# One tiny transfer issued by SyncE ahead of the first load of a batched matrix product

## The chip, the core and the metric

The kernel runs on one core of a Trainium2 chip. The metric is device time in microseconds (us) from launch to the last result in memory. A profiled execution also has a span, from the core's first to its last instruction.

## The reference

For each of 32 batch entries, a 256 x 512 matrix is multiplied by a 512 x 384 matrix, in float32:

```python
batch, dim_i, dim_j, dim_k = 32, 256, 512, 384
def reference(x, y):
    return np.einsum('bij,bjk->bik', x, y).astype(np.float32)
```

The inputs are 16.8 MB (x) and 25.2 MB (y), the output is 12.6 MB.

## The kernel before

**Tiling.** The 32 batch entries are taken in N = 8 groups of Q = 4. One group fills all 128 partitions, 32 partitions per entry. `load_x(n)` (line 67) brings the four x matrices of group n as one transfer of 128 rows of 16,384 bytes (2,048 KB). `load_y(n)` (line 71) brings the four y matrices as one transfer of 128 rows of 24,576 bytes (3,072 KB). Both inputs have two buffers, `x_sb[0..1]` and `y_sb[0..1]`, used by even and odd groups. The whole output of the core stays in one large tile `o_sb` until it is stored.

**Stages of one group.** GpSimd casts x (`round_x`, line 126) and y (`round_y`, line 136) from float32 to float16. VectorE transposes x blocks (line 156), TensorE multiplies (line 217) into PSUM, and ScalarE and VectorE copy the results from PSUM to `o_sb` (line 165). There is no planner: each engine's order is written out by hand, and the engines meet at semaphores.

**Transfers.** All of them are issued by SyncE, in one queue, which the profile calls q1. Four loads are issued at once, before the program branches to its bodies:

```python
for ins in (load_y(0), load_x(0), load_x(1), load_y(1)):
    tc.no_tile_sem_insts.add(ins.ins.name)
```

The other twelve loads (lines 98 to 102) each wait until the casts have emptied the buffer they write. Then come three stores (line 96): groups 0 to 4, groups 5 and 6, and group 7. `s_out` counts the landings of the stores, 16 for each transfer. The last instruction of the body waits for all of them and sets the semaphore back:

```python
sp.wait_op(s_out, 16 * 3, "sem-ge").then_inc(s_out, -16 * 3)
```

**What the steps below touch.** SyncE's order at the start (line 75), the queue q1 behind it, `s_out`, and everything that waits for `s_y[0]`: `round_y(0)` (line 136) is the first consumer of loaded data.

Of the kernel before, what the change touches and what calls it, by code (L numbers as in the profile page):

```python
# [9 lines left out]
F32 = mybir.dt.float32  # L10
P = 128
Q = 4
# [7 lines left out]
def kernel(  # L20
# [6 lines left out]
    nc = tc.nc  # L27

    B, I, J = x.shape
# [10 lines left out]
    def sbuf(name, shape, dtype):  # L40
        return nc.alloc_sbuf_tensor(name, shape, dtype).ap()
# [5 lines left out]
    xt_sb = sbuf("xt_sb", [P, TW, P], F32)  # L47
    y_r = sbuf("y_r", [P, T, K], MM_DT)
    spare = sbuf("spare", [1, 1], F32)
    o_ps = nc.alloc_psum_tensor("o_ps", [P, NE * Q, 512], F32).ap()  # L50

    s_x = [nc.alloc_semaphore(f"s_x{n}") for n in range(N)]
# [9 lines left out]
    s_out = nc.alloc_semaphore("s_out")  # L62
# [4 lines left out]
    def load_x(n):  # L67
        src = x[n * Q : (n + 1) * Q].rearrange("g (p r) j -> (g p) r j", r=R)
        return nc.sync.dma_start(out=x_sb[n % 2], in_=src).then_inc(s_x[n], 16)

    def load_y(n):
        src = y[n * Q : (n + 1) * Q].rearrange("g (q t) k -> (g q) t k", t=T)
        return nc.sync.dma_start(out=y_sb[n % 2], in_=src).then_inc(s_y[n], 16)

    for ins in (load_y(0), load_x(0), load_x(1), load_y(1)):
        tc.no_tile_sem_insts.add(ins.ins.name)
    tc.close()
    tc.compile()  # L78
# [12 lines left out]
    sp = nc.sync  # L91
# [16 lines left out]
    sp.wait_ge(s_dve, NE)  # L108
    store(N - 1, N)
    sp.sem_inc(s_sp, 1)  # L110
    sp.wait_op(s_out, 16 * 3, "sem-ge").then_inc(s_out, -16 * 3)

# [101 lines left out]
    def product(ps, w, m, start, stop, g):  # L216
        return te.add_instruction(  # L217
            mybir.InstMatmult(
                name=nc.get_next_instruction_name(),
                start_tensor_calc=start,  # L220
                stop_tensor_calc=stop,
                tile_size=(PQ, P),
                tile_position=(PQ * g, 0),
                engine=mybir.EngineType.PE,
                ins=[te.lower_ap(m), te.lower_ap(w)],
                outs=[te.lower_ap(ps)],
            )
        )

    xt = xt_sb.bitcast(MM_DT).rearrange("p t (m c) -> p t m c", c=2)  # L230
    with te.Fori(0, N):
        with te.Fori(0, NE) as e:
            take(s_act)
            take(s_dve)
            for t in range(T):
# [3 lines left out]
                for g in range(Q):  # L239
                    s = slice(g * PQ, (g + 1) * PQ)  # L240
                    ins = product(
                        o_ps[:, e * Q + g, :K],
                        xt[s, t // 2, :, t % 2],
                        y_r[s, t],
                        t == 0,
                        t == T - 1,
                        g,
                    )
# [32 lines left out]
```

## Time and profile before

| | us |
|---|---|
| median of 3 runs | 132.0 |
| lowest, highest | 131.71, 132.05 |
| the profiled execution, its own time | 132.13 |
| span of the profiled execution | 130.8 |

The 1.33 us between the profiled execution's time and its span lie outside the first and last instruction. The profile's rows that matter are quoted in the prediction. In the second part of the page the span is cut into 40 equal slices of 3.27 us and each digit is a share in tenths. "DMA" is the mean busy share of the core's 16 DMA engines. A row of the view by windows gives, for a stretch of the span, the busy time of each compute engine with the number of instructions in brackets, the granted TensorE clock, the DMA share and the rate in GB/s. The DMA share and the rate of a window count every packet that starts in it, with its whole duration and all of its bytes, so that a very short window shows one packet alone.

### The profile page before, as it was taken

The numbers are of one execution on the slowest core, as the hardware profiler recorded it, in microseconds if no ns is written. First come the engines' busy times: TensorE is split into PE (matmuls) and PEld (weight loads), VectorE is DVE, ScalarE is ACT, GpSimd is POOL, SyncE is SP. The second block draws the span as 40 slices with busy tenths as digits, with TensorE's granted clock in tenths as the row PEclk, the third lists the DMA queues.
The fourth block names the chain that finished last, engine by engine and source line by source line (L and its number), as shares of the span: only waits on it lengthen the run. The fifth ranks groups of instructions, "written<-read, shape, count | busy, mean of one in ns | idle before, by whom it ended". The sixth has DMA issues, their size and how long they took to land. (4 is left out here: it accounts for less than half of the span.)

```text
span 130.8 us, 3199 instructions
## 1 busy us (share of the span) xinstructions
PE 61.4 (47%) x1024; PEld 46.7 (36%) x1024; DVE 82.7 (63%) x144; ACT 84.1 (64%) x178; POOL 74.2 (57%) x42
## 2 busy tenths in 40 slices
PE   0000009910992589089329905980975499100000
PEld 0000009800991566046129604970953236000000
DVE  0000036899379999985997997599999957920000
ACT  0400000599659989993998899399999957994000
POOL 0006991199929965992899459758973970000000
PEclk9999999995589689977986985599599959965555
DMA  5999999999999999999999999999999999999995
GB/s 120 451 396 441 421 431 451 443 408 428 451 413 421 438 443 401 436 436 443 423 458 398 443 408 466 398 418 436 463 398 408 427 438 425 436 428 421 425 440 248
DMA packets 3379, 54.55 MB, mean 417 GB/s; under 512 B 304, under 2 KB 304, under 8 KB 304
## 3 DMA queue, kind: packets, MB, share of 16 engines
q1 hardware_dynamic: 3376, 54.53, 98.1%
q14 instruction: 3, 0.02, 0.0%
HBM read 41.94 MB, written 12.58 MB: 417 GB/s over the span
## 5 line engine op out<-in xcount | busy, mean ns | idle before, releaser
L165 ACT COPY o_sb<-o_ps (+1 forms) x176 | 82.6, 469 | 31.7 <-PE o_ps L217 29.6
L217 PE MATMUL o_ps<-y_r,xt_sb 32*128 32x384 f16 x1024 | 61.4, 384 | 50.4 <-PEq L214 49.5
L217 PEld LDWEIGHTS o_ps<-y_r,xt_sb 32*128 32x128 f16 x1024 | 46.7, 107 | 64.6 <-issue 56.8
L156 DVE STREAM_TRANSPOSE xt_sb<-x_r 128x256 f32<-128x256 f32 x64 | 38.1, 626 | 30.9 <-POOL x_r L126 18.4
L136 POOL CAST y_r<-y_sb 128x1536 f16<-128x1536 f32 (+1 forms) x22 | 44.3, 2049 | 15.8 <-DMA y_sb<-in_y_dram 15.3
L165 DVE COPY o_sb<-o_ps 32x384 f32 (+1 forms) x80 | 44.6, 557 | 1.6
L126 POOL CAST x_r<-x_sb 128x2048 f16<-128x2048 f32 x16 | 30.2, 1893 | 16.8 <-DVE o_sb L165 12.1
L202 ACT ACT_TABLE_LOAD x1 | 1.3, 1283 | 3.4 <-PEq L78 3.4
L265 POOL MEMSET const-float32-0.0<- 128x1 f32 x1 | 0.1, 98 | 0.2 <-issue 0.2
L202 ACT COPY spare<-const-float32-0.0 1x1 f32<-1x1 f32 x1 | 0.2, 190 | 0.0
L265 POOL MEMSET const-bfloat16-1.0<- 128x1 bf16 x1 | 0.1, 101 | 0.0
L265 POOL MEMSET const-uint8-127<- 128x1 uint8 x1 | 0.1, 101 | 0.0
L265 POOL MEMSET const-float32-1.0<- 128x1 f32 x1 | 0.1, 98 | 0.0
## 6 DMA issues: line engine op xcount, KB each, us to landing
y_sb<-in_y_dram SPq DMA_DIRECT2D x8, 3072.0 KB, 16.8
x_sb<-in_x_dram SPq DMA_DIRECT2D x8, 2048.0 KB, 17.0
out_dram<-o_sb SPq DMA_DIRECT2D x1, 7680.0 KB, 33.9
out_dram<-o_sb SPq DMA_DIRECT2D x1, 3072.0 KB, 17.3
out_dram<-o_sb SPq DMA_DIRECT2D x1, 1536.0 KB, 11.5
```

Of the source, the lines that this page charges most:

```text
L126: po.tensor_copy(x_r[:, e], x_sb[n % 2][:, e * H : (e + 1) * H]).then_inc(s_cast, 1)
L136: ins = po.tensor_copy(y_r[:, s], y_sb[n % 2][:, s])
L156: v.transpose(xt_w[:, w], words[:, e, w]).then_inc(s_xt, 1)
L165: ins = copy(o_sb[g * PQ : (g + 1) * PQ, n, e, h], o_ps[h * PQ : (h + 1) * PQ, e * Q + g, :K],)
L202: a_.copy(spare, nc.const_aps.tensor(0.0, [1, 1], F32))
L217: return te.add_instruction(mybir.InstMatmult(name=nc.get_next_instruction_name(), start_tensor_calc=start, stop_tensor_calc=stop, tile_si ...
L265: nc = _bacc.Bacc("TRN2", target_bir_lowering=False, num_devices=1)
```

## The change

SyncE issues one more transfer as its first instruction. It reads 16 rows of 64 bytes from group 0 of y, 128 rows of y apart, and writes them to a new tile `ahead` of 16 partitions, which nothing reads. It counts on `s_out`, so the final wait asks for 64 instead of 48. The tile is allocated behind all others in the on-chip memory, so no other tile moves. No other instruction of any engine changes or changes its place.

```diff
     spare = sbuf("spare", [1, 1], F32)
+    ahead = sbuf("ahead", [16, 16], F32)
     o_ps = nc.alloc_psum_tensor("o_ps", [P, NE * Q, 512], F32).ap()
...
-    for ins in (load_y(0), load_x(0), load_x(1), load_y(1)):
+
+    first = nc.sync.dma_start(
+        out=ahead, in_=y.rearrange("b j k -> (b j) k")[0 : Q * J : Q * J // 16, :16]
+    ).then_inc(s_out, 16)
+    for ins in (first, load_y(0), load_x(0), load_x(1), load_y(1)):
         tc.no_tile_sem_insts.add(ins.ins.name)
...
-    sp.wait_op(s_out, 16 * 3, "sem-ge").then_inc(s_out, -16 * 3)
+    sp.wait_op(s_out, 16 * 4, "sem-ge").then_inc(s_out, -16 * 4)
```

## The prediction

> **What bounds the kernel now.** I read the page first, for the shares by engine and the 40 slices, and look for an engine that is never idle.
>
> ```profile
> span 130.8 us, 3199 instructions
> PE 61.4 (47%) x1024; PEld 46.7 (36%) x1024; DVE 82.7 (63%) x144; ACT 84.1 (64%) x178; POOL 74.2 (57%) x42
> DMA  5999999999999999999999999999999999999995
> ...
> q1 hardware_dynamic: 3376, 54.53, 98.1%
> ...
> y_sb<-in_y_dram SPq DMA_DIRECT2D x8, 3072.0 KB, 16.8
> ...
> out_dram<-o_sb SPq DMA_DIRECT2D x1, 3072.0 KB, 17.3
> ```
>
> No compute engine is busy for more than 64% of the span. The DMA engines are at nine tenths or more in every slice but the first and the last. So the transfers bound the kernel. The view by windows says how the stream begins, runs and ends:
>
> ```profile
> core 0: us, PE busy (x) PEld busy (x) DVE busy (x) ACT busy (x) POOL busy (x), PEclk, DMA share, GB/s
> 0.00:1.75 1.75, 0.00 (x0) 0.00 (x0) 0.00 (x0) 0.00 (x0) 0.20 (x4) 1.00 0.00 0
> 1.75:2.75 1.00, 0.00 (x0) 0.00 (x0) 0.00 (x0) 0.00 (x0) 0.00 (x0) 1.00 1.70 393
> ...
> 2.75:3.25 0.50, 0.00 (x0) 0.00 (x0) 0.00 (x0) 0.00 (x0) 0.00 (x0) 1.00 0.00 0
> 4.25:10.00 5.75, 0.00 (x0) 0.00 (x0) 0.00 (x0) 0.67 (x2) 0.00 (x0) 1.00 1.00 430
> 10.10:10.90 0.80, 0.00 (x0) 0.00 (x0) 0.00 (x0) 0.00 (x0) 0.03 (x1) 1.00 0.91 389
> 3.25:129.25 126.00, 61.38 (x1024) 46.75 (x1024) 82.69 (x144) 84.10 (x178) 73.96 (x38) 0.82 1.00 429
> 130.30:130.31 0.01, 0.00 (x0) 0.00 (x0) 0.00 (x0) 0.00 (x0) 0.00 (x0) 0.50 0.06 0
> 130.31:130.80 0.49, 0.00 (x0) 0.00 (x0) 0.00 (x0) 0.00 (x0) 0.00 (x0) 0.50 0.00 0
> ```
>
> From 3.25 to 129.25 us the share is 1.00. Nothing is idle there that later work could use to catch up. The time is therefore the moment at which the engines get going, plus a fixed stream, plus a short tail. A microsecond that is lost or won at the start should arrive undiminished at the end. The other condition is that no transfer is issued too late. Here the median y load lands 16.8 us after its issue, while 3.146 MB at 430 GB/s take only 7.3 us: some 9 us of other packets stand ahead of it. The last store is covered as well, as SyncE's timeline shows:
>
> ```profile
> 109.82 9.80 SPq L96 DMA_DIRECT2D out_dram<-o_sb  x2
> ```
>
> These are the last two stores. The row begins with the issue of the second and ends at 109.82 + 9.80 = 119.62 us with the issue of the third. The second (3,072 KB) lands 17.3 us after its issue, near 127.1 us. So the third is queued some 7.5 us before the engines would run dry, and the compute chain ahead of it may be late by that much for nothing.
>
> **The start, packet by packet.** In 1.75 to 2.75 us 393 GB/s for 1 us are 393 KB, that is 16 packets of 24,576 bytes: one first packet of `load_y(0)` for each engine. Their durations add to 1.70 x 1.00 x 16 = 27.2 us, so one takes 1.70 us. In 4.25 to 10.00 us, 430 x 5.75 = 2,472 KB are 101 packets for 1.00 x 5.75 x 16 = 92 us, so one takes 0.91 us. The first packet of an engine thus costs 0.79 us more than a later one. Windows of 10 ns pick single ones out:
>
> ```profile
> 1.83:1.84 0.01, 0.00 (x0) 0.00 (x0) 0.00 (x0) 0.00 (x0) 0.00 (x0) 1.00 9.93 2458
> 1.95:1.96 0.01, 0.00 (x0) 0.00 (x0) 0.00 (x0) 0.00 (x0) 0.00 (x0) 1.00 13.38 2458
> 1.98:1.99 0.01, 0.00 (x0) 0.00 (x0) 0.00 (x0) 0.00 (x0) 0.00 (x0) 1.00 13.28 2458
> 2.55:2.56 0.01, 0.00 (x0) 0.00 (x0) 0.00 (x0) 0.00 (x0) 0.00 (x0) 1.00 9.43 2458
> ```
>
> Each holds one packet (2458 GB/s for 10 ns are 24.6 KB), and share x 0.01 x 16 is its duration: 1.59, 2.14, 2.12 and 1.51 us. They end near 3.42, 4.09, 4.11 and 4.06 us. So the slowest engines begin their steady run 0.7 us after the quickest.
>
> **The change part by part.** It removes nothing. It adds one issue on SyncE, 16 data packets and 16 semaphore packets in q1, one more count for the last wait, and it moves SyncE's first four loads behind the new issue.
>
> ```profile
> 0.74 0.39 SPq L73 DMA_DIRECT2D y_sb<-in_y_dram  x1
> 1.18 0.90 SPq L69 DMA_DIRECT2D x_sb<-in_x_dram  x2
> 2.12 0.53 SPq L73 DMA_DIRECT2D y_sb<-in_y_dram  x1
> 20.27 0.33 SPq L69 DMA_DIRECT2D x_sb<-in_x_dram  x1
> ```
>
> *The issue.* SyncE issues in order and its first issue starts at 0.74 us. The second starts at 1.18, so the price of standing in front is 0.44 us. Bounds are 0.33 us (the issue at 20.27) and 0.53 us (the one at 2.12). I take 0.44, since it is the first issue of the same engine in the same place. `load_y(0)` then moves from 0.74 to 1.18, and its first packets, which started just behind 1.75 us (no window before that holds one), come near 2.2 us. What waits for y, GpSimd's first cast and all behind it, moves with it by the same 0.44 us, and so do the later loads, which wait for those casts; by the 9 us in which a load queues, that is covered. Two x loads and `load_y(1)` are issued 0.44 us later too. These cost nothing, as 3,072 KB of y stand in front of them; if that cover were gone, it would be the same 0.44 us.
>
> *The packets.* A semaphore packet costs 0.06 x 0.01 x 16 = about 0.01 us (window 130.30 to 130.31). No row shows a packet of 64 bytes. At 27 GB/s, the rate of an engine in the steady windows (430/16), it would be 2 ns, and an isolated first one may cost as much as the whole excess, 0.79 us. Between these ends the question is what the excess is. It may be the time in which an idle engine waits for its first data. Then the tiny packet has it and `load_y(0)`, coming 0.44 us later with its own request, has it again, side by side: net +0.44 us. Or it may be a cost of an engine's very first packet alone. Then the tiny packet pays for it while SyncE is still issuing, and the net is 0.44 - 0.79 = -0.35 us. For the latest engines, whose excess is 2.14 - 0.91 = 1.23 us, it is -0.79 us. Or the two follow strictly one after the other, and the net is up to 0.44 + 0.79 = +1.23 us. The trace has one row on new addresses. The first packets of `load_x(0)`, in 10.10 to 10.90 us, take 0.91 x 16 / 389 = 0.0374 ns per byte, against 16 / 430 = 0.0372 before them. So an address that is new does not by itself cost a running engine anything. It does not say whether an engine with one 64-byte packet behind it counts as running. I take the first reading, as it needs no state that outlives a packet.
>
> The Trainium skill, on the page "Perfetto Trace Analysis" (section "DMA Instruction — HWDGE (DVE, Sync)"), speaks against the change: the closing semaphore write of a transfer goes out only after the write before it is confirmed. If the engine's later packets were held meanwhile, it would be the strictly serial case below. The steady windows disagree: semaphore packets stand among their data packets, and the share is still 1.00.
>
> *The final wait and the tile.* The tiny transfer lands over 100 us before the last wait looks at `s_out`, so 64 costs what 48 did. Nothing else is touched.
>
> *The sum.* Span 130.8 + 0.44 = 131.24 us, plus the 1.33 us around it (132.13 - 130.8) makes 132.57 us, which is +0.44 on the profiled execution. That execution stands 0.13 us above the median of 132.0. On the median it makes 132.4 us.
>
> **The rivals.**
>
> *The engines are woken early (faster).* The mechanism is that the excess is paid once per engine, at its first packet, and the tiny transfer pays it. For: the excess is large, it appears nowhere else in 126 us, and the latest three engines of the start, not the mean, have the most to win. Against: the four packets above started up to 0.7 us apart and still finished in two bunches, near 3.4 and 4.1 us, so part of it is waiting and not a fee. Net -0.35 us by the mean and -0.79 us for the latest engines, so 131.65 to 131.2 us; about 131.4. It decides from a fee above 0.44 us on.
>
> *The delay is absorbed (no change).* If all engines wait for something which the first request sets going, the tiny transfer sets it going at the old moment, 1.75 us. `load_y(0)` at 2.2 us would still be in time, since the early engines' data flows only from 3.42 - 0.91 = 2.5 us on. Net 0: 132.0 us. It speaks for this that a packet which started at 2.55 ended no later than one that started at 1.98. The same time would come out if the transfer did not do what it says, but hit only a few of the engines and left the issue hidden.
>
> *Strictly one after the other (slower still).* The tiny packet keeps each engine until its data are written and told. The trace's measure of the latter is the tail: from the last semaphore packet at 130.30 to the end, 0.5 us. The engines are then free at 1.75 + 0.79 + 0.5 = 3.04 us in place of 1.75, and pay the first excess again: +1.3 us, 133.3 us; with half of it overlapped, 132.7. Against it stand the steady windows, where nothing is held.
>
> **How the numbers follow.** The one-to-one delay has a chance of 0.44, the woken engines 0.29, the absorbed delay 0.12, the serial case 0.15. About 0.3% (0.4 us) is what a measurement of this kernel can tell from no change. The delay of 0.44 us lies just above that bound, so I give three quarters of its chance to slower (0.33) and a quarter to same (0.11). The serial case is slower throughout (0.15). Of the woken engines 0.25 is faster, 0.04 same. The absorbed delay is same (0.12). So faster 0.25, same 0.27, slower 0.48. The likeliest case alone spans 132.2 to 132.6 (bounds of the issue, 0.33 to 0.53, and the spread of the runs shown). The range reaches to 131.3 for most of the woken case and to 132.9 for the half-overlapped serial case; left out are the far ends of both.
>
> **What would show it.** Right: SyncE's timeline shows the new issue near 0.74 us and `load_y(0)` near 1.18; the window of the first 24 KB packets begins near 2.2 us; their mean stays near 1.7 us; and the steady share begins 0.4 us later than 3.25. Woken engines would show first y packets near 0.9 us and a steady run that begins no later than before. An absorbed delay would show means near 1.3 us. The serial case would show first packets from 2.6 us on or later. The forecast is wrong if the first y packets end earlier than 3.4 to 4.1 us, or if the end does not move with the start.

## The result, and the profile after

The changed kernel takes 132.40 us (median of 22 runs, 132.28 to 133.13) against 132.01 us for the kernel before (22 runs, 131.71 to 132.59). The ratio is 1.0034, with a 95% interval of 1.0023 to 1.0045: it is slower by 0.30 to 0.59 us, and the forecast was 132.4 us.

The page of the profiled execution (132.40 us) shows a picture much like the one before:

```profile
span 131.1 us, 3200 instructions
PE 65.2 (50%) x1024; PEld 52.9 (40%) x1024; DVE 82.4 (63%) x144; ACT 84.1 (64%) x178; POOL 74.1 (57%) x42
DMA  4899999999999999999999999999999999999996
...
q1 hardware_dynamic: 3408, 54.53, 97.9%
...
ahead<-in_y_dram SPq DMA_DIRECT2D x1, 1.0 KB, 1.5
```

There is one instruction more, 32 packets more (3,408 against 3,376), and the DMA row is nine tenths or more from the third slice to the last but one. It differs from the row before at its two ends: 4 and 8 where 5 and 9 stood, and 6 where 5 stood. The stream lies later by a part of a slice. SyncE's timeline (start, duration, issue) shows by how much:

```profile
0.74 0.39 SPq L77 DMA_DIRECT2D ahead<-in_y_dram  x1
1.19 0.41 SPq L74 DMA_DIRECT2D y_sb<-in_y_dram  x1
1.65 0.90 SPq L70 DMA_DIRECT2D x_sb<-in_x_dram  x2
```

The tiny transfer has taken the place at 0.74 us, and the first load is issued at 1.19 instead of 0.74: 0.45 us later. The windows of the changed kernel (last two columns: DMA share and GB/s) show the rest of the start:

```profile
1.70:2.00 0.30, 0.00 (x0) 0.00 (x0) 0.00 (x0) 0.00 (x0) 0.00 (x0) 1.00 0.06 4
2.20:3.20 1.00, 0.00 (x0) 0.00 (x0) 0.00 (x0) 0.00 (x0) 0.00 (x0) 1.00 1.55 393
3.20:3.65 0.45, 0.00 (x0) 0.00 (x0) 0.00 (x0) 0.00 (x0) 0.00 (x0) 1.00 0.00 0
3.65:129.65 126.00, 65.22 (x1024) 52.91 (x1024) 82.42 (x144) 84.10 (x178) 73.85 (x38) 0.82 1.00 429
```

The 16 tiny packets and their 16 semaphore packets all start in 1.70 to 2.00 us and take 0.06 x 0.30 x 16 = 0.29 us together, 9 ns each. They are gone before the first packets of y appear. Those 16 (393 KB in 1 us) start from 2.20 us on, where they had started from 1.75 on, and take 1.55 us on average (1.55 x 1.00 x 16 / 16), against 1.70 us before. The steady stretch of 126 us has the same share (1.00) and the same rate (429 GB/s) as before. How much later the stream lies is shown by windows of 10 ns, the first of the kernel before, the other two of the changed one:

```profile
3.41:3.42 0.01, 0.00 (x0) 0.00 (x0) 0.00 (x0) 0.00 (x0) 0.00 (x0) 1.00 5.76 2458
3.65:3.66 0.01, 0.00 (x0) 0.00 (x0) 0.00 (x0) 0.00 (x0) 0.00 (x0) 1.00 5.70 2458
130.57:130.58 0.01, 0.00 (x0) 0.00 (x0) 0.00 (x0) 0.00 (x0) 0.00 (x0) 0.50 0.06 0
```

The first packet behind the first 16 starts at 3.65 us instead of 3.41, and the last semaphore packet at 130.57 us instead of 130.30. In this pair of executions the stream is 0.24 us late at its start and 0.27 us late at its end, so nothing was caught up in between. That is less than the 0.45 us of the issue; the first packets, shorter by 0.15 us on average, would account for most of the difference. Between the medians it is 0.39 us.

The compute engines did not carry the delay to the end. The row of the last two store issues ends at 110.20 + 9.30 = 119.50 us with the issue of the last one, against 119.62 us before:

```profile
110.20 9.30 SPq L101 DMA_DIRECT2D out_dram<-o_sb  x2
```

TensorE was busy 3.8 us longer than before (65.2 against 61.4 us), but that does not go with the time: two_ahead below is slower still and has 61.2 us.

### The profile page after: what moved, and what is told of

Its sections match the earlier page's. It is cut to its first block, busy times and chain, and to the rows that moved or that the text cites. A ratio compares the mean times of both kernels' runs of the same rounds, so it can differ in the third digit from the quotient of the medians.

```text
span 131.1 us, 3200 instructions
## 1 busy us (share of the span) xinstructions
PE 65.2 (50%) x1024; PEld 52.9 (40%) x1024; DVE 82.4 (63%) x144; ACT 84.1 (64%) x178; POOL 74.1 (57%) x42
## 3 DMA queue, kind: packets, MB, share of 16 engines
q1 hardware_dynamic: 3408, 54.53, 97.9%
## 5 line engine op out<-in xcount | busy, mean ns | idle before, releaser
L222 PE MATMUL o_ps<-y_r,xt_sb 32*128 32x384 f16 x1024 | 65.2, 405 | 46.9 <-PEq L219 43.7
L222 PEld LDWEIGHTS o_ps<-y_r,xt_sb 32*128 32x128 f16 x1024 | 52.9, 112 | 58.8 <-issue 52.4
```

What stands on the lines that cost most here:

```text
L222: return te.add_instruction(mybir.InstMatmult(name=nc.get_next_instruction_name(), start_tensor_calc=start, stop_tensor_calc=stop, tile_si ...
```

## The experiments

Three theories were to be told apart. *Issue time:* the price is the time that SyncE spends on one more issue ahead of the first load. *Packets:* it is the 32 additional packets or the count on `s_out`. *Waking:* a part of what the issue costs is given back, because the tiny transfer takes the engines' first excess on itself (1.55 against 1.70 us looked like it). In each group the kernels were compared with runs of the kernel before on the same chip. For the first four kernels below the kernel before had a median of 131.96 us, for the other four 131.97 us. The diffs are cut to the lines that matter. In them `tiny(engine)` issues the tiny transfer on the named engine.

**behind_y0: the same transfer, issued second.**

```diff
-    for ins in (first, load_y(0), load_x(0), load_x(1), load_y(1)):
+    for ins in (load_y(0), tiny(nc.sync), load_x(0), load_x(1), load_y(1)):
```

> The same tiny transfer, but issued second, behind load_y(0). Theory 1 (the price is SyncE's issue time in front of the first load): load_y(0) is issued at 0.74 us again, its first packets start near 1.77 us, and the time is that of before, 132.0 us (within 0.15), although x(0), x(1) and y(1) are issued 0.44 us later. Theory 2 (the price is the 32 extra packets and the one more count on s_out): the time stays at 132.4 us.

It took 132.06 us, ratio 1.0008 [0.9999, 1.0017]: not different from before. Timeline and window of this kernel:

```profile
0.74 0.39 SPq L74 DMA_DIRECT2D y_sb<-in_y_dram  x1
1.19 0.41 SPq L78 DMA_DIRECT2D ahead<-in_y_dram  x1
1.66 0.94 SPq L70 DMA_DIRECT2D x_sb<-in_x_dram  x2
```

```profile
1.75:2.75 1.00, 0.00 (x0) 0.00 (x0) 0.00 (x0) 0.00 (x0) 0.00 (x0) 1.00 1.68 393
```

The packets and the count are all there, and so is the 0.45 us of issue, now in front of the x loads (1.66 against 1.18 us). Only the first load is back at 0.74 us, and the time is back too. So behind the first load the packets cost nothing that can be measured (at most 0.22 us by the interval), and here an issue costs time only in front of the transfer that starts the stream.

**two_ahead: two tiny transfers ahead of the first load.**

```diff
-    for ins in (first, load_y(0), load_x(0), load_x(1), load_y(1)):
+    for ins in (tiny(nc.sync, ahead), tiny(nc.sync, ahead2), load_y(0), load_x(0), load_x(1), load_y(1)):
```

> Two tiny transfers ahead of load_y(0). Theory 1 (issue time): load_y(0) is issued near 1.64 us (0.74 + 2 x 0.45), the first 24 KB packets start near 2.65 us, the time is 132.0 + 2 x 0.42 = 132.85 us. Rival (a part of the first packets' excess is a fee that the first tiny transfer has already paid, which is why after is 0.39 and not 0.45): the second one saves nothing more, so it adds its full 0.45 and the time is 132.4 + 0.45 = 132.85 too, with a mean first y packet as in after (1.55 us); if the mean falls again to about 1.4 us, the saving is not a fee but overlap with waiting.

It took 133.02 us, ratio 1.0086 [1.0072, 1.0100], which is 0.95 to 1.32 us slower. Its timeline and window:

```profile
0.74 0.86 SPq L80 DMA_DIRECT2D ahead<-in_y_dram  x2
1.65 0.41 SPq L74 DMA_DIRECT2D y_sb<-in_y_dram  x1
```

```profile
2.65:3.65 1.00, 0.00 (x0) 0.00 (x0) 0.00 (x0) 0.00 (x0) 0.00 (x0) 1.00 1.69 393
```

The first load is 0.91 us late (1.65 - 0.74), which is just below the interval; a little more was lost than the delay alone. The mean first packet is back at 1.69 us. If a tiny transfer saved the excess, two would not save less than one, so the 1.55 us of the changed kernel does not look like one.

**ahead_from_act: the tiny transfer in ScalarE's queue, SyncE as before.**

```diff
-    for ins in (first, load_y(0), load_x(0), load_x(1), load_y(1)):
+    for ins in (tiny(nc.scalar), load_y(0), load_x(0), load_x(1), load_y(1)):
```

> The tiny transfer issued by ScalarE in its own queue at the start, SyncE's order as before. Theory 1 (issue time on SyncE): load_y(0) at 0.74 us again and the time is 132.0 us (within 0.15). If both issues share one descriptor generator, one holds the other up and part of the 0.44 us comes back (132.0 to 132.4 us). Rival (waking pays): the engines have their first packet a little earlier than y's, mean first y packet under 1.5 us, time under 131.8 us.

It took 132.06 us, ratio 1.0006 [0.9997, 1.0016]. The timeline, and the issues with their time to landing:

```profile
0.74 0.39 SPq L73 DMA_DIRECT2D y_sb<-in_y_dram  x1
0.74 0.41 ACTq L78 DMA_DIRECT2D ahead<-in_y_dram  x1
1.19 0.90 SPq L70 DMA_DIRECT2D x_sb<-in_x_dram  x2
```

```profile
ahead<-in_y_dram ACTq DMA_DIRECT2D x1, 1.0 KB, 5.0
```

```profile
0.00:1.75 1.75, 0.00 (x0) 0.00 (x0) 0.00 (x0) 0.00 (x0) 0.20 (x4) 1.00 0.00 0
1.75:2.75 1.00, 0.00 (x0) 0.00 (x0) 0.00 (x0) 0.00 (x0) 0.00 (x0) 1.00 1.83 393
2.75:3.30 0.55, 0.00 (x0) 0.00 (x0) 0.00 (x0) 0.00 (x0) 0.00 (x0) 1.00 0.00 0
```

Both engines issue at 0.74 us, the first load loses nothing, and neither does the kernel. The tiny transfer lands 5.0 us after its issue, against 1.5 us when it stood first. By the windows (the last rows), y's 16 first packets make up the 393 KB of 1.75 to 2.75 us, and nothing else starts before 3.30. So the tiny packets came after y's first ones here and could not have woken anything. The run bears out the issue time and says nothing on waking.

**wait_for_landing: a wait for the tiny transfer's landing.**

```diff
     ).then_inc(s_out, 16)
+    nc.sync.wait_ge(s_out, 16)
```

> The tiny transfer ahead, and SyncE waits for its landing before it issues load_y(0). Theory A (the excess of the first packets is the wait of an empty engine for its first data, paid whenever the engine is empty): load_y(0) is issued near 0.74 + 1.5 = 2.2 us, its first packets start near 3.25 us and take 1.6 to 1.7 us again on average; time 132.0 + 1.5 = 133.5 us. Theory B (it is a fee of an engine's first packet alone): the first y packets take about 0.95 us, time 133.5 - 0.75 = 132.8 us.

This one missed its aim. The wait came to stand at `load_x(0)`, behind `load_y(0)`, as SyncE's waits show (waited in total, times, longest):

```profile
SPq L70 <- DMA ahead<-in_y_dram: 0.6, 1, 0.6
```

```profile
1.19 0.41 SPq L74 DMA_DIRECT2D y_sb<-in_y_dram  x1
2.23 0.92 SPq L70 DMA_DIRECT2D x_sb<-in_x_dram  x2
```

So `load_y(0)` was issued at 1.19 us as in the changed kernel (the second fence is its timeline), and only the x loads were later, at 2.23 us. It took 132.48 us, ratio 1.0037 [1.0024, 1.0051], as the changed kernel did. It shows at least that x loads a further 0.6 us late cost nothing behind 3,072 KB of y.

**landed_first and loads_in_body: the wait where it was meant to be, and its control.** The four first loads move into SyncE's body; in landed_first they stand behind the wait, in loads_in_body there is no tiny transfer.

```diff
-    for ins in (first, load_y(0), load_x(0), load_x(1), load_y(1)):
-        tc.no_tile_sem_insts.add(ins.ins.name)
+    tc.no_tile_sem_insts.add(first.ins.name)
...
+    sp.wait_ge(s_out, 16)
+    load_y(0)
+    load_x(0)
+    load_x(1)
+    load_y(1)
     for n in range(2, N):
```

> The wait for the tiny transfer's landing again, this time in front of load_y(0): in wait_for_landing the wait came to stand behind that load, at load_x(0). Here the four first loads are issued in SyncE's body, behind the wait. Theory A (the excess of the first packets is the wait of an empty engine for its first data): load_y(0) near 2.25 us, first packets near 3.3 us, mean duration 1.55 to 1.85 us as in all runs so far; time 132.0 + 1.5 = 133.5 us. Theory B (a fee of an engine's first packet alone, which the tiny one has paid): mean near 0.95 us, time near 132.8 us.

> The control of landed_first: no tiny transfer, the four first loads in SyncE's body. Both theories: load_y(0) is issued behind the branch, near 1.2 to 1.6 us, mean first y packet near 1.7 us, time 132.0 plus the delay of the issue (132.5 to 132.9 us).

landed_first took 133.62 us, ratio 1.0127 [1.0109, 1.0146]. Its timeline and windows:

```profile
0.74 0.39 SPq L77 DMA_DIRECT2D ahead<-in_y_dram  x1
2.40 0.35 SPq L74 DMA_DIRECT2D y_sb<-in_y_dram  x1
```

```profile
1.70:2.20 0.50, 0.00 (x0) 0.00 (x0) 0.00 (x0) 0.28 (x1) 0.00 (x0) 1.00 0.03 2
3.35:4.45 1.10, 0.00 (x0) 0.00 (x0) 0.00 (x0) 0.06 (x1) 0.00 (x0) 1.00 1.46 357
```

Here every engine's tiny packet was over by 2.20 us and its landing was known before y was issued, a full second start 1.66 us after the first. The 16 first packets of y (357 x 1.10 = 393 KB) still take 1.46 x 1.10 x 16 / 16 = 1.61 us. The excess is thus no fee for an engine's first packet of all. It comes back, on average, when the empty engines get their first large packets. The whole 1.66 us is lost at the end (1.44 to 1.93 us by the interval).

The control took 132.70 us, ratio 1.0049 [1.0034, 1.0064], with its first load at 1.39 us:

```profile
1.39 0.39 SPq L73 DMA_DIRECT2D y_sb<-in_y_dram  x1
```

That is a delay of 0.65 us without any tiny transfer, and 0.45 to 0.84 us are lost. The loss goes with the delay, whatever makes it.

**one_row and rows_128: what the issue costs by the number of rows.**

```diff
-        out=ahead, in_=y.rearrange("b j k -> (b j) k")[0 : Q * J : Q * J // 16, :16]
+        out=ahead[0:1], in_=y.rearrange("b j k -> (b j) k")[0:1, :16]
```

rows_128 has `[0 : Q * J : Q * J // 128, :16]` and a tile of 128 partitions in its place.

> The transfer ahead reads one row of 64 bytes in place of 16, so that it runs on one engine. If the price is a fixed time of an issue: load_y(0) still near 1.19 us, time 132.4 to 132.45 us as with 16 rows. If it goes by the number of packets: load_y(0) near 0.8 us, time 132.0 us.

> The transfer ahead reads 128 rows of 64 bytes in place of 16, 8 packets for each engine. If the price is a fixed time of an issue: load_y(0) near 1.19 us and 132.4 to 132.5 us. If it goes by packets, or if small packets hold the engines, clearly above 132.6 us.

One row took 132.41 us, ratio 1.0028 [1.0018, 1.0039]; 128 rows took 132.41 us, ratio 1.0032 [1.0021, 1.0043]. The timelines of one_row and of rows_128:

```profile
0.74 0.35 SPq L77 DMA_DIRECT2D ahead<-in_y_dram  x1
1.14 0.37 SPq L74 DMA_DIRECT2D y_sb<-in_y_dram  x1
```

```profile
0.74 0.39 SPq L77 DMA_DIRECT2D ahead<-in_y_dram  x1
1.18 0.42 SPq L74 DMA_DIRECT2D y_sb<-in_y_dram  x1
```

The first load is issued at 1.14 and at 1.18 us. From 1 to 128 rows the price of standing in front stays between 0.40 and 0.45 us. It is a price per issue. The queue's packets in one_row and in rows_128 are these:

```profile
q1 hardware_dynamic: 3378, 54.53, 97.3%
q1 hardware_dynamic: 3520, 54.54, 97.7%
```

Against 3,376 before, that is 2 and 144 more, where 16 rows brought 32: one packet for each row, and 1, 16 and 16 semaphore packets. The time is 132.40 or 132.41 us with all three, so the packets in front cost nothing measurable either. The 16 semaphore packets fit a transfer that runs on all 16 engines, on which the reading of landed_first rests.

## Why the prediction was right

**The bound.** The stream of transfers sets the time, with no slack in 126 us. That held. Kernels that delay the first load by 0.40 to 1.66 us lose about their delay:

| kernel | first load issued at, us | delay, us | ratio, 95% interval | lost, us |
|---|---|---|---|---|
| behind_y0 | 0.74 | 0 | 0.9999 to 1.0017 | -0.01 to 0.22 |
| one_row | 1.14 | 0.40 | 1.0018 to 1.0039 | 0.24 to 0.51 |
| after | 1.19 | 0.45 | 1.0023 to 1.0045 | 0.30 to 0.59 |
| loads_in_body | 1.39 | 0.65 | 1.0034 to 1.0064 | 0.45 to 0.84 |
| two_ahead | 1.65 | 0.91 | 1.0072 to 1.0100 | 0.95 to 1.32 |
| landed_first | 2.40 | 1.66 | 1.0109 to 1.0146 | 1.44 to 1.93 |

(lost = (ratio - 1) x 132.0 us; rows_128 and wait_for_landing, with delays of 0.44 and 0.45 us, lie beside the changed kernel.) In two_ahead alone the loss lies above the delay, by at least 0.04 us.

**The issue.** Taken from the old distance between the first and the second issue, 0.44 us; it measured 0.45 us. This was the whole sum, and the row that was chosen among three was the right one.

**The packets.** Put between 2 ns and 0.79 us, and taken at nothing; they measured 9 ns each, and behind_y0 shows that they cost nothing measurable.

**The excess of the first packets.** The forecast took the reading that an idle engine waits for its first data, that the tiny packet has this wait, and that `load_y(0)` has it again. Only the last part came true, on average: 1.55 us in the changed kernel, and 1.61 us in landed_first, where the tiny transfer had landed. The tiny packets, the first on idle engines, took 9 ns each and show no such wait. Nor does every first packet of y have the excess. The one that started last took 5.68 x 0.01 x 16 = 0.91 us, as long as a packet of the stream, in the kernel before, in the changed kernel and in landed_first:

```profile
2.62:2.63 0.01, 0.00 (x0) 0.00 (x0) 0.00 (x0) 0.00 (x0) 0.00 (x0) 1.00 5.68 2458
3.16:3.17 0.01, 0.00 (x0) 0.00 (x0) 0.00 (x0) 0.00 (x0) 0.00 (x0) 1.00 5.68 2458
4.43:4.44 0.01, 0.00 (x0) 0.00 (x0) 0.00 (x0) 0.00 (x0) 0.00 (x0) 1.00 5.68 2458
```

In ahead_from_act the one that started last took 2.44 us, so a late start alone does not spare the excess. Neither a wait of each idle engine nor a fee of each first packet fits. What makes the earlier ones longer stays open. That the excess did not change the sum was right; the reason given for it was not, and there the forecast was lucky.

**The rivals.** Woken engines would have shown y packets near 0.9 us, and they took 1.55 us. The absorbed delay needed a mean near 1.3 us, and both the delay and the end moved. The strictly serial case is out as well: y's first packets started at 2.20 us, 0.45 later than before, and not after 2.6. The prediction also named the Trainium skill for it, "Perfetto Trace Analysis" (section "DMA Instruction — HWDGE (DVE, Sync)"): the closing semaphore write of a transfer goes out only after the write before it is confirmed. The tiny packets and their semaphore packets started in one 0.3 us window, at 9 ns each, and y's came as long after their own issue as before (2.20 - 1.19 = 1.01 us, and 1.75 - 0.74 = 1.01 us). So whatever the semaphore write waits for, it did not hold the engines' later packets.

**What the forecast had nearly wrong.** It named a mean of 1.7 us for y's first packets, and the changed kernel showed 1.55 us. Read by itself that is a third of the delay won back. The other profiles show 1.61 to 1.83 us (1.83 in ahead_from_act, where the time was that of before). The five kernels with tiny packets for 16 engines ahead of y average 1.66 us, the four without any ahead of it 1.74 us. One execution of each does not tell these two apart, so 1.55 us may be the spread between executions, and a saving of about 0.1 us is neither shown nor excluded.


## What to carry to other kernels

Where the profile shows the transfers busy from end to end, the time from launch to the first large transfer's packets is on the path undiminished, as here; keep the issue of that transfer first on its engine and put anything small behind it or on another engine's queue. A warm-up transfer costs a whole issue (0.40 to 0.45 us here, for 1 to 128 rows), and it has to be shown that it saves more than that: look at the durations of the first large packets, over several profiles, before believing in it. No kernel tried here was faster than the kernel before.

## What had not been expected

Issued at the same moment from ScalarE's queue, the 1 KB transfer landed 5.0 us after its issue instead of 1.5 us: although the two queues are separate in the profile (q10 with 32 packets beside q1), the tiny packets came after y's first large ones.

Single first packets can be much longer than the mean. In the profiled executions of one_row (133.22 us) and rows_128 (132.91 us), both kernels with a median of 132.41 us, two windows of 10 ns with one packet each show 17.54 x 0.01 x 16 = 2.81 us and 17.39 x 0.01 x 16 = 2.78 us:

```profile
2.13:2.14 0.01, 0.00 (x0) 0.00 (x0) 0.00 (x0) 0.00 (x0) 0.00 (x0) 1.00 17.54 2458
2.47:2.48 0.01, 0.00 (x0) 0.00 (x0) 0.00 (x0) 0.00 (x0) 0.00 (x0) 1.00 17.39 2458
```

In the other eight profiles the longest first packet took 1.96 to 2.44 us, and the execution lay within 0.12 us of its kernel's median. So the two executions that ran long are the two with the longest first packets. That a long one puts off the whole stream of its engine, and so the end, would explain them, but it was not tried by itself.
